# The y products of the RWKV steps, grouped by tile shape

## The chip, the cores and the metric

The kernel runs on one core of a Trainium2 chip. Its time is the device time of one execution in microseconds; the number that stands for a kernel is the median of its runs. The span is the time from the first to the last instruction of one profiled execution.

## The reference

One encoder layer on 256 tokens of width 2048, all in fp32. A combined projection of the normalised input feeds three things: a differential-attention group, an RWKV-7 group of 16 heads of 64 channels, and two merge gates. The two branches are projected, merged and added to the residual. Then a mixture of 16 experts with 32 tokens each follows.

The change lies in the RWKV-7 group. Each head has a 64x64 state S, scanned over the tokens once forward and once backward, and the two outputs are added:

```python
def step(S, inp):
    r_t, w_t, k_t, v_t, a_t, b_t = inp
    sa = jnp.einsum('bhvk,bhk->bhv', S, a_t)
    S = S * w_t[:, :, None, :] + sa[..., None] * b_t[:, :, None, :] + v_t[..., None] * k_t[:, :, None, :]
    return S, jnp.einsum('bhvk,bhk->bhv', S, r_t)
```

## The kernel before, in words

The scan is done in chunks of 64 tokens, four in sequence. Within a chunk the recurrence is solved with a triangular inverse, so a chunk needs a few matmuls of 64 columns. Heads are taken in four groups (`gp`, lines 612 to 630). A group has two head pairs (e), two heads per pair (h, in partitions 0 to 63 and 64 to 127, the slices `HH`), and two directions (d): eight scans side by side, which the list `eh` (line 533) runs through with h innermost.

For each group, three projections (`project_c`, lines 229 to 245) give r, k and v; `prep` (line 372) forms decays, the keys and the operands `X`, `rb`, `bt`, `vt_`; `invert` (line 474) forms `tt`, mainly by 62 small VectorE operations in sequence. `chain` (line 528) then runs the four sequential steps for the group before. A step c does the following:

- prr (line 557): eight products of the state tile `ss_` with `X[..., 0]`; ScalarE copies them to `rh` (559).
- pu (567): eight products of `tt` and `rh`; ScalarE and VectorE copy one head half each into `uu` (568, 569).
- psn (573), not in the last step: eight products of `bt` and `uu`; with the decayed state they become the next state `nsu` (574 to 580).
- py (583, 584): for each of the eight scans a product of `ss_` with `X[..., 1]`, contraction over 128 partitions, and then a product of `uu` with `rb`, contraction over 64 partitions, added to it. The two directions are then copied to `y` by ScalarE in steps 0 and 1 and added to it by VectorE in steps 2 and 3 (587, 589).

In the profile the first kind is the form 128\*64 (rows by columns of the array), the second 64\*64. Each fp32 matmul shows as two records, so eight matmuls are "x16".

prr, pu, psn and py are tiles of one PSUM pool, `chp`, with two banks (line 67). A new tile takes a bank when one is free, and an instruction that needs it waits until then. All eight banks of PSUM are given out to the pools of lines 63 to 67.

The order of the instructions on each engine is made when the kernel is built: a planner goes through them by priority and by its own model of their times (line 1013), and adds the semaphores. Weights' splits have priority 9000, `prep` and `invert` of group gp 10000 + 4000 gp, the chains 16000 and a term that grows with gp; a lower number goes first. The large projections, those of r, k and v and of the merge gates (`gates`, `GSCHED`), come behind all of these and fill the places between them. At run time each engine works through its own list in that order.

The projections' weights come through SyncE's queue in chunks of 512 KB and are split into a high and a low half (`wsplit`, lines 198 to 209) by ScalarE and VectorE (205, 206), two buffers for each half. After the RWKV groups come the attention, the branch projections, the output projection, the routing, and the experts (from line 882), whose weights are 1 MB loads into a ring of buffers (line 179).

Of the kernel before, what the change touches and what calls it, by code (L numbers as in the profile page):

```python
# [8 lines left out]
F32 = mybir.dt.float32  # L9
# [23 lines left out]

GSCHED = (1, 4, 1, 4, 6)    # gate projections behind each group of RWKV heads, and behind the last one
PS, PCH = 9000, 16000       # scheduling priorities: weights' splits; the heads' chunks in sequence
NEW, NE1, NEB = 14, 2, 8    # slots for the experts' weights: a ring, those of it free early, those used once
PACE = 3                    # chunks of other weights per early load of the experts'

# [14 lines left out]
def trunk_kernel(ctx, tc, x, attn_norm_g, w_in, q_norm_g, k_norm_g, lambda_q1, lambda_k1, lambda_q2,  # L53
# [4 lines left out]
    V, A, G, PE, SP = nc.vector, nc.scalar, nc.gpsimd, nc.tensor, nc.sync  # L58
# [8 lines left out]
    chp = tc.alloc_tile_pool(name="chp", bufs=2, space=PSUM)  # L67
# [37 lines left out]
    with ExitStack() as es:  # L105
# [29 lines left out]
        for kp in range(KT // 2):  # L135
# [5 lines left out]
            for i in range(2):  # L141
                kt = 2 * kp + i
                g = prm[:, 100 + kt:101 + kt]
# [3 lines left out]
    def pieces(q):  # L147
        """column pieces of the down projections; narrow ones at the very end"""
        return ((0, 1024), (1024, 1024)) if q < 3 else ((0, 1024), (1024, 512), (1536, 256), (1792, 256))
# [15 lines left out]
    def slot_of(i):  # L165
        """the pool of load i: the ring of NEW slots (NE1 of them free early), or the NEB that serve once"""
        if NEW <= i < NEW + NEB:
            return 2
        return int((i if i < NEW else i - NEB) % NEW >= NE1)
# [18 lines left out]
    def pace(wl):  # L188
        """ahead of the experts, a load of their weights for every few chunks of the stream"""
        i = len(ew_state["tiles"])  # L190
        if i == NEW or ew_state["pools"][slot_of(i)] is None:
            return
        ew_state["chunks"] += 1
        if ew_state["chunks"] % PACE == 0:
            with prio(2000000 + ew_state["chunks"]):
                fetch(wl[0:1, 0:1].bitcast(F32))
# [16 lines left out]
    def project_t(src, nk, c0, lh, ll, name, pool=None):  # L213
        """tokens on partitions: two banks [128 tok, 512]"""
        pool, tag = pool or (pjp, "pj")
        ps = [pool.tile([128, 512], F32, name=f"pj_{name}_{t}", tag=tag) for t in range(2)]
        for kc in range(nk // 2):
            wh, wl = wsplit(src[:, 2 * kc:2 * kc + 2, c0:c0 + 512], 2, 512, f"{name}_{kc}")
            for j in range(2):
                kt = 2 * kc + j  # L220
                for t in range(2):
                    s = slice(t * 128, (t + 1) * 128)
                    first, last = kt == 0, kt == nk - 1
                    PE.matmul(ps[t], lh[:, kt, s], wh[:, j], start=first, stop=False)  # L224
                    PE.matmul(ps[t], lh[:, kt, s], wl[:, j], start=False, stop=False)  # L225
                    PE.matmul(ps[t], ll[:, kt, s], wh[:, j], start=False, stop=last)  # L226
        return ps

    def project_c(src, nk, c0, width, rh, rl, name, pool=None):
        """channels on partitions: one bank [<=128 ch, 256 tok] per 128 columns"""  # L230
        nct = (width + 127) // 128
        pool, tag = pool or (pjp, "pj")
        ps = [pool.tile([128, T], F32, name=f"pc_{name}_{c}", tag=tag) for c in range(nct)]
        for kc in range(nk // 4):
            wh, wl = wsplit(src[:, 4 * kc:4 * kc + 4, c0:c0 + width], 4, width, f"{name}_{kc}")
            for c in range(nct):
                m = min(128, width - c * 128)
                for j in range(4):
                    kt = 4 * kc + j
                    first, last = kt == 0, kt == nk - 1  # L240
                    cs = slice(c * 128, c * 128 + m)
                    PE.matmul(ps[c][:m], wh[:, j, cs], rh[:, kt], start=first, stop=False)  # L242
                    PE.matmul(ps[c][:m], wh[:, j, cs], rl[:, kt], start=False, stop=False)  # L243
                    PE.matmul(ps[c][:m], wl[:, j, cs], rh[:, kt], start=False, stop=last)  # L244
        return ps
# [15 lines left out]

# [1 line left out]
    with ExitStack() as es:  # L263
# [71 lines left out]
        def head_norm(src, npair, scale, lo, eps, tag, pl_, pt_):  # L335
            """per-token, per-head rsqrt(max-or-add) of channel sums, spread back over the channels"""
            def tmp_(i):
# [34 lines left out]
        def prep(G_, e, r, k, v):  # L372
# [9 lines left out]
            SP.dma_start(w2s[64:128, 1], a2_b[0, :, chs])  # L382
            # decay and in-context rate
            pw = prepp.tile([128, 2, T], F32, name=f"pw{p}", tag="pr")
# [7 lines left out]
            for d in range(2):  # L392
                A.activation(ta[:, d], pa[:, d], AF.Tanh, bias=pch(44 + 8 * d), scale=0.5)
            # normalised keys
            kkr = r1.tile([128, T], F32, name="kkr", tag="kkr")
# [12 lines left out]
            V.tensor_copy(dec[:, 4:8], pp_[:, 4:8, 1])  # L408
            # the state's side of X: a | r of each head in its own half
            for h, hs in enumerate(HH):  # L410
# [11 lines left out]
            V.tensor_tensor(bk[:, :, 1], c8(ta), c8(cum), op=OP.mult)  # L422
            # products within the chunks: ab | rb in the head's half, ak | rk in the other half of X
            # (ab transposed for the backward scan)
            for d in range(2):
# [18 lines left out]
                for h in range(2):  # L444
                    ks = HH[1 - h]
                    V.tensor_tensor(X[ks, h, ns].rearrange("p n w t -> p n (w t)"), pK[ks],
                                    mk[ks, :, 128:256].to_broadcast([64, 4, 128]), op=OP.mult)
            # bonus, with the group norm's bias
            G.tensor_tensor(z, ta[:, 0], ta[:, 1], op=OP.add)
# [4 lines left out]
            G.tensor_scalar(z, z, pc(92), 1.0, op0=OP.add, op1=OP.mult)  # L454
            # values, and keys scaled to the chunk's end, with time on partitions
            pv = prepp.tile([128, 4, 64], F32, name=f"pv{p}", tag="pr")
# [17 lines left out]
        def invert(G_):  # L474
            """unit-triangular inverses: 32-blocks by substitution, blocks and row residues on partitions"""
            g, ab, tt = G_["g"], G_["ab"], G_["tt"]
# [51 lines left out]
        def chain(G_):  # L528
            """chunks in sequence, four scans side by side, then group norm, bonus and gate"""
            g = G_["g"]  # L530
# [4 lines left out]
            def stacked(c, name, eng):  # L535
                """a state's or a u's tile, the values of step c in its other half"""
                t = r2.tile([128, 2, 2, 2, 64], F32, name=name, tag=name)
# [6 lines left out]
            ss_, sd = None, None  # L544
            for c in range(4):
# [10 lines left out]
                for e, h, d in eh:  # L556
                    PE.matmul(prr[HH[h], e, d], X[:, e, h, ii[d], 0], ss_[:, e, h, d], start=True, stop=True)
                rh = r1.tile([128, 2, 2, 64], F32, name="rh")
                A.copy(rh, prr)
                if 0 < c < 3:  # L560
# [9 lines left out]
                if c < 3:  # L570
# [3 lines left out]
                    for h, hs in enumerate(HH):  # L574
# [4 lines left out]
                        else:  # L579
                            A.copy(nsu[hs, :, h], psn[hs])  # L580
                py = chp.tile([128, 2, 2, 64], F32, name=f"py{g}_{c}", tag="ch")
                for e, h, d in eh:
                    PE.matmul(py[HH[h], e, d], ss_[:, e, h, d], X[:, e, h, ii[d], 1], start=True, stop=False)
                    PE.matmul(py[HH[h], e, d], uu[HH[h], e, h, d], rb[HH[h], e, ii[d]], start=False, stop=True)
                for d in range(2):
# [51 lines left out]

# [1 line left out]
    hres = tc.alloc_tile_pool(name="hres", bufs=1, side=right)  # L639
# [7 lines left out]

# [1 line left out]
    ybr = tc.alloc_tile_pool(name="ybr", bufs=1, side=right)  # L649
# [18 lines left out]

# [1 line left out]
    with ExitStack() as es:  # L670
# [111 lines left out]

# [1 line left out]
    mg = tc.alloc_tile_pool(name="merged", bufs=1, side=left)  # L784
# [12 lines left out]

# [1 line left out]
    h = hrow  # L799
# [32 lines left out]

# [1 line left out]
    rt_ = ctx.enter_context(tc.tile_pool(name="route", bufs=1, side=left))  # L834
# [46 lines left out]

# [1 line left out]
    with ExitStack() as es:  # L883
        ewb = tc.alloc_tile_pool(name="ewb", bufs=NEB, side=left)
        ew_state["pools"][2] = ewb
        for q in range(4):
            es_ = slice(4 * q, 4 * q + 4)
            # one-hot rows of the slots: rstd folded in for the gather, the affinity for the scatter
            oh = e2.tile([128, 2, 4, CAP], F32, name="oh")
# [127 lines left out]
```

## Time and profile before

| what | us |
|---|---|
| median of three runs | 1905.14 |
| lowest and highest run | 1902.57, 1911.13 |
| span of the profiled execution | 1908.2 |
| TensorE busy (share) | 1718.0 (90%) |
| VectorE busy (share) | 702.0 (37%) |
| ScalarE busy (share) | 440.8 (23%) |
| GpSimd busy (share) | 192.7 (10%) |

The profiled execution is listed with its span alone, no other time of its own. The page is read from the totals down to single instructions: which engine is busy in which stretch, what it waits for there, and then the instructions that the change touches, one after another in order of time.

### The profile page before, as it was taken

To read this page: it belongs to the slowest core of one execution; us is meant where nothing else is said; L and a number is where in the kernel's file an instruction comes from. 1 tells how busy PE (TensorE), PEld (TensorE's weight loads), DVE (VectorE), ACT (ScalarE), POOL (GpSimd) and SP (SyncE) were. 2 spreads that over 40 slices of the span, in tenths; PEclk is the share of its full clock that TensorE was granted. 3 is DMA by queue.
4 is the path that set the end of the run, shared out by engine and by line. 5 is a ranking of instruction groups with operands and counts; after the bars stand their busy time and mean duration, and the time that the engine had idled before them with its cause. 6 is when DMAs were issued, how large, how long until landed. Compare 5 with 4: busy or idle time off the path is not lost.

```text
span 1908.2 us, 27455 instructions
## 1 busy us (share of the span) xinstructions
PE 1718.0 (90%) x11179; PEld 1059.7 (56%) x11179; DVE 702.0 (37%) x1524; ACT 440.8 (23%) x768; POOL 192.7 (10%) x295
## 2 busy tenths in 40 slices
PE   6999999999998899999979988978889888878877
PEld 6988888888987677998845222322223222211123
DVE  4678777696634667775430010000000000000000
ACT  6444444343333456544410000000000000000000
POOL 2342213332000331000000000000000000000000
PEclk9999999999999999999989999999999999999989
DMA  5655634355545665688899999999999999999997
GB/s 164 176 142 153 166 101 122 95 141 150 143 129 177 178 185 166 208 252 277 281 366 414 423 421 423 427 427 426 421 423 427 427 425 420 424 427 427 425 417 271
DMA packets 230383, 556.49 MB, mean 292 GB/s; under 512 B 40954, under 2 KB 138736, under 8 KB 197232
## 3 DMA queue, kind: packets, MB, share of 16 engines
q1 hardware_dynamic: 229904, 554.68, 78.7%
q8 instruction: 88, 1.44, 0.3%
q14 instruction: 39, 0.32, 0.0%
q0 software_dynamic: 352, 0.05, 0.0%
HBM read 543.14 MB, written 11.53 MB: 291 GB/s over the span
## 4 chain that ended last, share of the span: by engine, by line
DMA 36%; PE 25%; SPq 2%; DVE 1%; issue 1%; ACT 0%; POOL 0%; ACTq 0%; POOLq 0%; DVEq 0%
DMA w<-in_w_down_e_dram 13%; DMA w<-in_w_gate_e_dram 12%; DMA w<-in_w_up_e_dram 10%; PE pgu L920 5%; PE pd L954 4%; SPq L179 2%; PE pc_br L242 2%; PE pc_br L244 2%; PE pxe L903 2%; PE pc_br L243 2%; PE pj_wo L225 1%; PE pj_wo L226 1%; PE pj_wo L224 1%; PE pj_da L225 1%; PE pj_da L224 1%; PE pj_da L226 1%
## 5 line engine op out<-in xcount | busy, mean ns | idle before, releaser
L920 PE MATMUL pgu<-w,xe 128*32 128x512 f32 x2048 | 453.9, 603 | 65.8 <-DMA w<-in_w_gate_e_dram 32.5
L920 PEld LDWEIGHTS pgu<-w,xe 128*32 128x32 f32 x2048 | 109.8, 110 | 393.7 <-issue 230.2
L954 PE MATMUL pd<-w,hdT 128*32 128x512 f32 (+1 forms) x1088 | 245.4, 592 | 56.5 <-DMA w<-in_w_down_e_dram 55.6
L954 PEld LDWEIGHTS pd<-w,hdT 128*32 128x32 f32 x1088 | 64.7, 111 | 233.7 <-DMA w<-in_w_down_e_dram 122.9
L242 PE MATMUL pc_gt<-xh,wh_gt 128*128 128x256 f32 x512 | 149.7, 295 | 0.0
L244 PE MATMUL pc_gt<-xh,wl_gt 128*128 128x256 f32 x512 | 144.8, 294 | 5.2 <-DVE wl_gt L206 5.0
L243 PE MATMUL pc_gt<-xl,wh_gt 128*128 128x256 f32 x512 | 146.6, 289 | 0.0
L935 ACT ACTIVATE th<-pgu 128x512 f32<-128x512 f32 x8 | 4.8, 597 | 519.0 <-PE pgu L920 519.0
L904 DVE TENSOR_TENSOR xe<-pxe,fg 128x512 f32<-128x512 f32 x16 | 11.0, 690 | 295.0 <-PE pgu L920 241.7
L242 PE MATMUL pc_rkv<-xh,wh_rkv 128*128 128x256 f32 x384 | 111.1, 292 | 2.0 <-ACT wh_rkv L205 2.0
L243 PE MATMUL pc_rkv<-xl,wh_rkv 128*128 128x256 f32 x384 | 111.8, 293 | 0.0
L244 PE MATMUL pc_rkv<-xh,wl_rkv 128*128 128x256 f32 x384 | 108.5, 293 | 1.1 <-DVE wl_rkv L206 1.1
L963 DVE TENSOR_TENSOR acc<-poe,acc 128x512 f32<-128x512 f32 (+1 forms) x26 | 16.9, 651 | 247.3 <-PE poe L962 247.3
L244 PEld LDWEIGHTS pc_gt<-xh,wl_gt 128*128 128x128 f32 x512 | 96.7, 194 | 9.4 <-DVE wl_gt L206 7.0
L242 PEld LDWEIGHTS pc_gt<-xh,wh_gt 128*128 128x128 f32 x512 | 99.7, 195 | 3.3 <-issue 1.2
L243 PEld LDWEIGHTS pc_gt<-xl,wh_gt 128*128 128x128 f32 x512 | 99.9, 195 | 1.6 <-issue 1.1
L936 DVE SCALAR_TENSOR_TENSOR th<-th,pgu 128x512 f32<-128x512 f32 x8 | 5.5, 688 | 249.8 <-ACT th L935 216.4
L206 DVE TENSOR_TENSOR wl_gt<-raw_gt,wh_gt 128x1024 fp32r<-128x1024 f32 x64 | 79.7, 1246 | 43.2 <-ACT wh_gt L205 43.1
L205 ACT CAST wh_gt<-raw_gt 128x1024 fp32r<-128x1024 f32 x64 | 67.0, 1046 | 100.3 <-PE pc_gt L243 81.4
L225 PE MATMUL pj_da<-wl_da,xh 128*128 128x512 f32 x192 | 78.4, 408 | 6.9 <-DVE wl_da L206 6.8
L958 ACT COPY ye<-pd 128x512 f32<-128x512 f32 (+1 forms) x17 | 9.5, 561 | 311.0 <-PE pd L954 311.0
L206 DVE TENSOR_TENSOR wl_da<-raw_da,wh_da 128x1024 fp32r<-128x1024 f32 x48 | 63.6, 1324 | 37.7 <-ACT wh_da L205 37.2
(385 smaller groups left out, 2964.8 us busy)
## 6 DMA issues: line engine op xcount, KB each, us to landing
w<-in_w_gate_e_dram SPq DMA_DIRECT2D x128, 1024.0 KB, 19.5
w<-in_w_up_e_dram SPq DMA_DIRECT2D x128, 1024.0 KB, 19.6
w<-in_w_down_e_dram SPq DMA_DIRECT2D x128, 1024.0 KB, 18.1
raw_gt<-in_w_in_dram SPq DMA_DIRECT2D x64, 512.0 KB, 3.9
raw_rkv<-in_w_in_dram SPq DMA_DIRECT2D x48, 512.0 KB, 3.9
raw_da<-in_w_in_dram SPq DMA_DIRECT2D x48, 512.0 KB, 3.7
raw_wo<-in_w_out_dram SPq DMA_DIRECT2D x32, 512.0 KB, 5.5
raw_br<-in_w_branch_b_dram SPq DMA_DIRECT2D x16, 512.0 KB, 4.0
```

Of the source, the lines that this page charges most:

```text
L179: SP.dma_start(w, src)
L205: A.copy(wh[:, :n], raw[:, :n])
L206: V.tensor_tensor(wl[:, :n], raw[:, :n], wh[:, :n].bitcast(F32), op=OP.subtract)
L224: PE.matmul(ps[t], lh[:, kt, s], wh[:, j], start=first, stop=False)
L225: PE.matmul(ps[t], lh[:, kt, s], wl[:, j], start=False, stop=False)
L226: PE.matmul(ps[t], ll[:, kt, s], wh[:, j], start=False, stop=last)
L242: PE.matmul(ps[c][:m], wh[:, j, cs], rh[:, kt], start=first, stop=False)
L243: PE.matmul(ps[c][:m], wh[:, j, cs], rl[:, kt], start=False, stop=False)
L244: PE.matmul(ps[c][:m], wl[:, j, cs], rh[:, kt], start=False, stop=last)
L903: PE.matmul(px[:, j], h[:, t, kt::KT], ohr[:, t], start=t == 0, stop=t == 1)
L920: PE.matmul(pgu[2 * gu + hf][js], xe[kt // 4][:, kt % 4, js], wt[2 * j + gu][:, k, hf * 512:(hf + 1) * 512], start=kt == 0, stop=kt == KT - 1)
L954: PE.matmul(pd[nb][js], hT[:, ft, js], wt[j][:, k, nb * nw:(nb + 1) * nw], start=ft == 0, stop=ft == 7)
```

## The change

The state products of a step are issued right behind prr, as one run of eight; the u products stay in their place behind psn, as a second run of eight. The bank of py is therefore taken at the start of the step. The start flag, which clears a bank's marks for the partitions that the matmul writes, is set only on the first two state products (one in each half of the partitions), and the stop flag on the last two u products. Operands, outputs and the number of matmuls are the same. The diff also drops comments and docstrings, which is not shown.

```diff
                 for e, h, d in eh:
                     PE.matmul(prr[HH[h], e, d], X[:, e, h, ii[d], 0], ss_[:, e, h, d], start=True, stop=True)
                 rh = r1.tile([128, 2, 2, 64], F32, name="rh")
+                py = chp.tile([128, 2, 2, 64], F32, name=f"py{g}_{c}", tag="ch")
+                for k_, (e, h, d) in enumerate(eh):
+                    PE.matmul(py[HH[h], e, d], ss_[:, e, h, d], X[:, e, h, ii[d], 1], start=k_ < 2, stop=False)
                 A.copy(rh, prr)
...
-                py = chp.tile([128, 2, 2, 64], F32, name=f"py{g}_{c}", tag="ch")
-                for e, h, d in eh:
-                    PE.matmul(py[HH[h], e, d], ss_[:, e, h, d], X[:, e, h, ii[d], 1], start=True, stop=False)
-                    PE.matmul(py[HH[h], e, d], uu[HH[h], e, h, d], rb[HH[h], e, ii[d]], start=False, stop=True)
+                for k_, (e, h, d) in enumerate(eh):
+                    PE.matmul(py[HH[h], e, d], uu[HH[h], e, h, d], rb[HH[h], e, ii[d]], start=False, stop=k_ > 5)
                 for d in range(2):
                     if c < 2:
                         A.copy(y[:, :, nn[d]], py[:, :, d])
```

## Rows read from the trace of the kernel before

**Rows 1.** The page, totals: engine, busy us, share of the span, instructions.

```profile
span 1908.2 us, 27455 instructions
PE 1718.0 (90%) x11179; PEld 1059.7 (56%) x11179; DVE 702.0 (37%) x1524; ACT 440.8 (23%) x768; POOL 192.7 (10%) x295
```

**Rows 2.** Busy time by stretch: length, PE, PEld, DVE, ACT, POOL, clock, DMA share, GB/s.

```profile
140.00:220.00 80.00, 75.18 (x752) 69.09 (x751) 67.74 (x161) 35.05 (x58) 16.41 (x21) 1.00 0.64 170
220.00:600.00 380.00, 374.49 (x3879) 330.71 (x3879) 252.61 (x580) 142.25 (x255) 82.88 (x123) 0.97 0.47 125
300.00:500.00 200.00, 195.87 (x2106) 172.41 (x2099) 144.51 (x338) 73.72 (x135) 51.40 (x76) 0.97 0.46 122
...
1040.00:1908.00 868.00, 732.87 (x3134) 215.01 (x3134) 42.65 (x66) 19.70 (x36) 0.00 (x0) 0.98 1.00 415
```

**Rows 3.** Waits of PE, 200 to 1000 us: total us, times, longest.

```profile
PE pj_da L225 <- DVE wl_da L206: 6.8, 4, 3.9
...
PE pc_gt L244 <- DVE wl_gt L206: 2.6, 4, 1.2
```

**Rows 4.** Chain of waits, a stretch of the experts: start us, us, what.

```profile
1222.01 19.56 DMA w<-in_w_up_e_dram
```

**Rows 5.** Timeline of PE, one step's y products: start us, us, line, out<-in.

```profile
256.09 0.33 PE L583 MATMUL py<-X,su 128*64 128x64 f32 x2
256.35 0.33 PE L584 MATMUL py<-rb,uu 64*64 64x64 f32 x2
...
259.68 0.50 PE L244 MATMUL pc_rkv<-xh,wl_rkv 128*128 128x256 f32 x2
```

**Rows 6.** Busy time by stretch, instructions on the tile py alone: PE, PEld, DVE, ACT.

```profile
220.00:600.00 380.00, 67.35 (x512) 48.75 (x512) 3.99 (x16) 3.46 (x16) 0.97 0.47 125
```

**Rows 7.** Timeline of PE, psn and the instruction behind it.

```profile
223.85 0.69 PE L573 MATMUL psn<-uu,bt 128*64 128x64 f32 x16
224.36 0.28 PE L583 MATMUL py<-X,su 128*64 128x64 f32 x2
```

**Rows 8.** Timeline of PE, prr and pu, each with the instruction behind it.

```profile
262.14 0.69 PE L557 MATMUL prr<-su,X 128*64 128x64 f32 x16
...
262.75 0.39 PE L244 MATMUL pc_rkv<-xh,wl_rkv 128*128 128x256 f32 x1
...
265.34 0.68 PE L567 MATMUL pu<-rh,tt 64*64 64x64 f32 x16
...
265.95 0.33 PE L583 MATMUL py<-X,su 128*64 128x64 f32 x2
...
266.21 0.38 PE L244 MATMUL pc_rkv<-xh,wl_rkv 128*128 128x256 f32 x1
```

**Rows 9.** Tile py: ns min/median/max of an instruction; who waited for it (us, times).

```profile
L583 PE MATMUL py<-X,su x256: 222/222/367, 224.4 to 582.5; 128*64 128x64 f32 x128
...
  ACT su L541: 24.9, 8
```

**Rows 10.** Stretches with line 583 alone: PE, PEld, clock; first and last of four.

```profile
240.00:250.00 10.00, 2.55 (x16) 1.43 (x14) 0.83 0.14 38
...
540.00:550.00 10.00, 0.00 (x0) 0.00 (x0) 0.83 0.32 84
```

**Rows 11.** Timeline of PE, projections behind a block of y products, and later.

```profile
244.83 0.41 PE L244 MATMUL pc_rkv<-xh,wl_rkv 128*128 128x256 f32 x1
245.04 0.41 PE L242 MATMUL pc_rkv<-xh,wh_rkv 128*128 128x256 f32 x1
...
247.77 0.28 PE L243 MATMUL pc_rkv<-xl,wh_rkv 128*128 128x256 f32 x1
247.88 0.28 PE L244 MATMUL pc_rkv<-xh,wl_rkv 128*128 128x256 f32 x1
```

**Rows 12.** Waits of DVE, 220 to 600 us: total us, times, longest.

```profile
DVE wl_rkv L206 <- ACT wh_rkv L205: 17.1, 11, 6.9
DVE y L589 <- PE py L584: 14.0, 6, 3.2
```

## The prediction

> **What bounds the kernel now.** I read the page's totals first. TensorE is busy for 1718 of the 1908.2 us [rows 1], but that is a mean over stages with different limits, so the second view is the busy time by stretch. The changed lines run only between 224 and 583 us. From 220 to 600 us PE is busy 374.5 of 380 us, while DVE has 252.6 and ACT 142.3, and the DMA share is 0.47 [rows 2]. The third view asks what PE waits for: from 200 to 1000 us the longest entry in the list is 6.8 us, and the largest wait inside the changed stretch is 2.6 us for the low halves of the gate weights [rows 3]. So in this stretch PE is the bound, and PE time that is really removed moves everything behind it forward.
>
> From 1040 us on the DMA engines are full at a share of 1.00 and PE has 733 of 868 us [rows 2]; the chain of waits there is one expert weight after another, 19.56 us each [rows 4]. That stage is as long as its bytes. It doesn't hide a gain made before it, because its loads wait for buffers and code that come after the RWKV stage: it begins sooner and lasts as long. A gain in 220 to 600 us should reach the end nearly whole.
>
> **The y products today.** Each of the 16 steps (4 groups by 4 chunks) issues 8 pairs: a state product on the 128\*64 form (line 583), then a u product on the 64\*64 form (line 584). Each matmul is two fp32 passes, so a step is 16 pieces "x2". In the timeline the pieces alternate and start 0.256 us apart: from 256.09 to 259.68 us there are 14 pieces, 3.59 us [rows 5]. One step thus holds PE for 16 x 0.256 = 4.10 us, and 16 steps for 65.6 us. The busy time of the tile py gives 67.35 us from the other side; it counts the tail of each last matmul [rows 6]. A few pieces continue a run of the same form before them and cost less, so I take 65.
>
> **The same matmuls in one form.** Three products of the same step show it. The 16 passes of psn (128\*64) start at 223.85 and the next same-form instruction at 224.36: 0.51 us [rows 7]. Those of prr (128\*64) start at 262.14 and a projection follows at 262.75: 0.61 us. Those of pu (64\*64) start at 265.34, and the next form at 265.95: 0.61 us [rows 8]. These are exactly the two forms of the y products, with the same moving size of 64 columns. The price today is therefore the change of form between pieces, not the arithmetic: a single pass has the same median of 0.222 us in the alternation [rows 9].
>
> **What the change does to it.** The number of matmuls stays at 16 passes of each form per step; no copy is added.
> - First run (state products): it now stands right behind prr, which reads the same state and has the same form. Between 0.51 us (joined to prr) and 0.61 us (alone). I take 0.55.
> - Second run (u products): 0.61 us if whole. The planner cuts runs today where half of u comes late; one pair cut off and surrounded by projections holds 0.26 us, as at 265.95 us [rows 8]. So 0.61 to 0.87, and I take 0.70, nearer the whole run, since pu is whole in the same place.
> - Sum per step 1.25 us, for 16 steps 20 us. Removed: 65 - 20 = 45 us. Bounds: 65.6 - 16 x 1.12 = 47.7 and 65 - 16 x 1.48 = 41.3 us.
> - The start flag on two matmuls in place of eight, and the stop flag, change no instruction; I cost them at nothing, because flags ride on matmuls that are issued anyway.
>
> The two heads' u products sit in different row halves of the array and write one bank; pu does the same today, and its 16 passes leave room for the next form after 0.61 us [rows 8]. The Trainium skill ("TensorEngine Tiling (Array Packing)", Restrictions and Gotchas) says that different row tiles cannot access the same PSUM bank simultaneously, and that software must keep them apart. By the row the second run costs 0.61 us, by that rule up to 16 x 0.22 = 3.5 us. The trace doesn't bear the rule out for tiles that also lie in different column halves, and I go by the row.
>
> **The clock.** In five places the granted clock is at its lower level, 1.2 GHz, for a part of a slice: slices at 0.83 in 240 to 250, twice in 350 to 370, 490 to 500 and 540 to 550 us [rows 10]. Each begins at the end of, or within half a microsecond behind, a block of alternating y products; the projections behind the first then start 0.21 us apart in place of 0.12 [rows 11]. A slice at 0.83 loses 1.7 us, so five cost 8.5. The uniform runs of 0.6 us don't show this in their wake. Without the 4 us blocks I expect most of it back: 0 to 8.5 us, I take 6.
>
> **What is late next.** PE gets 51 us less work in 380, so other engines come closer. In the densest part, 300 to 500 us, DVE has 144.5 us of work; the eight steps of two groups run there, so 200 - 8 x 2.8 - 5 (three of the clock's places) = 173 us remain, 84% DVE. The nearest case is 140 to 220 us: DVE 67.7 of 80 us (85%), and PE is busy 75.2 there, 6% lost [rows 2]. If that held over 300 to 500 us, some 10 us would be lost; if the cover holds, as now, nothing. I take 6.
>
> **The moved waits.** ACT waits 24.9 us in 8 places for the state products before it can refill a state buffer [rows 9]; with the products early, these go. ACT isn't the bound, so I count nothing. The added wait: py now takes one of the pool's two banks from the start of the step to the y copies, where pu took it before. pu must wait for rh's copy out of prr's bank, psn for u's copy out of pu's bank; both wait for that data today. Only the next step's first run waits for something new, the y copies. Queued behind it on PE are pu and the projections. Today DVE stands ready for the y sums and waits for PE, 14.0 us in 6 places [rows 12], so the copies come at once; nothing counted.
>
> **Sum.** -45 - 6 + 6 = -45 us. The profiled span is 1908.2 us, 3.1 above the median of 1905.14, and no other time is listed for that execution; 1908.2 - 45 = 1863.2 there, and 1860 beside the median.
>
> **Rivals.**
> - Half is lost (0.09): the order on every queue is planned anew at build, and DVE, with its splits, falls behind PE; DVE already waits for ACT, 6.9 us at the longest [rows 12]. For: 84% DVE. Against: DVE's waits are mostly for engines that wait for PE. Gain 23 us, 1882.
> - The change doesn't do what it says (0.06): the planner cuts the runs into pairs between projections. Each pair then costs a change of form, 0.26 us again, and only half the clock loss returns: 1896 to 1907, say 1901. Against: prr and pu, traced the same way, are mostly whole.
> - The late bank (0.05), the slower side: the first run stands in PE's order ahead of pu, and if the y copies sit on DVE behind a split that waits for ACT, PE stands still in the 12 steps that have one before them. It decides from 51 / 12 = 4.3 us per step; at 5.5 us it is 66 us and the time 1905 - 51 + 66 = 1920. Against: [rows 12] shows DVE early.
> - Row halves kept apart in one bank (0.02): 16 x (3.5 - 0.7) = 45 us of the gain go, about 1905.
>
> **How the numbers follow.** The forecast has 0.78; its own spread is 1848 (all 47.7 and 8.5 us, no new wait) to 1876 (41.3, no clock, 10 us of waits, and the spread of the runs shown, 1902.6 to 1911.1). To hold eight in ten with some weight for the second case the range is 1848 to 1884. A measurement can tell 0.5% (9.5 us) from no change. Faster: 0.78 + 0.09 + half of 0.06 = 0.90; same 0.03 + 0.02 = 0.05; slower 0.05.
>
> **What would show it.** Right: tile py busy near 22 us for 512 passes (32 runs of 0.69 us, the last tail counted), rows "x16" or longer for both lines, the slices at 0.83 gone or fewer, PE still above 93% until the RWKV steps end, and the stage from the first expert weight to the end as long as now. Wrong: pieces "x2" in the y products, PE waits for low halves or for y copies of more than 15 us in total, or an expert stage that grew by what the front lost.

## The result and the profile after

The changed kernel takes 1878.32 us (median; 1875.99 to 1878.9) beside 1908.14 us for the kernel before on the same chip: ratio 0.9842, 95% interval 0.9824 to 0.9861. The forecast was 1860 us in 1848 to 1884. The direction and the main term were right; the gain is 30 us in place of 45.

The page of the changed kernel, totals (columns as in [rows 1]):

```profile
span 1876.0 us, 27452 instructions
PE 1679.5 (90%) x11179; PEld 1032.0 (55%) x11179; DVE 701.4 (37%) x1524; ACT 440.4 (23%) x768; POOL 189.9 (10%) x295
```

PE has as many instructions as before and 38.5 us less busy time. The span is 32.2 us shorter, so somewhere PE also gained idle time.

The timeline of PE, one step of the changed kernel, answers to [rows 5], [rows 7] and [rows 8]:

```profile
311.34 0.69 PE L557 MATMUL prr<-su,X 128*64 128x64 f32 x16
311.86 0.64 PE L563 MATMUL py<-X,su 128*64 128x64 f32 x16
312.43 1.13 PE L390 MATMUL pa<-lora,w2s 128*128 128x512 f32 x2
```

```profile
255.31 0.67 PE L587 MATMUL py<-rb,uu 64*64 64x64 f32 x14
255.92 0.39 PE L243 MATMUL pc_rkv<-xl,wh_rkv 128*128 128x256 f32 x1
```

The first run joins prr, 0.52 us behind its start, and gives way after 0.57 us. The second holds PE for 0.61 us, here without one pair (x14). That pair stands ahead of it between projections and holds PE for 0.25 us by itself:

```profile
252.46 0.32 PE L587 MATMUL py<-rb,uu 64*64 64x64 f32 x2
252.71 0.39 PE L244 MATMUL pc_rkv<-xh,wl_rkv 128*128 128x256 f32 x1
```

The second run is cut in this way in 14 of the 16 steps. The two forms of the y products do not alternate any more. Busy time on the tile py alone (answers to [rows 6]; it begins at 130 us, because the first step's state products are now issued at 140 us):

```profile
130.00:600.00 470.00, 27.57 (x512) 21.53 (x512) 3.91 (x16) 3.48 (x16) 0.97 0.54 148
```

67.35 has become 27.57 us. To see what became of these 39.8 us, both traces are read over two stretches: from 101 us to the end of the gate projections, and from the start to the first expert matmul. First the kernel before, then the changed one; columns as in [rows 2]:

```profile
101.00:588.00 487.00, 474.97 (x4935) 424.54 (x4934) 342.75 (x774) 190.92 (x339) 115.82 (x163) 0.98 0.50 132
...
0.00:982.60 982.60, 928.50 (x7701) 815.46 (x7702) 654.94 (x1451) 420.71 (x731) 192.70 (x295) 0.97 0.59 175
```

```profile
101.00:562.00 461.00, 434.49 (x4937) 398.56 (x4936) 345.66 (x790) 190.30 (x338) 113.88 (x163) 0.97 0.52 140
...
0.00:949.60 949.60, 884.64 (x7700) 785.02 (x7700) 654.50 (x1451) 420.30 (x731) 189.88 (x295) 0.98 0.61 181
```

Up to the end of the gates PE is busy 40.5 us less (474.97 to 434.49), and idle 14.5 us more (12.0 to 26.5): the stretch is 26.0 us shorter. But it is not quite the same work: the last matmuls of the last head group start at 599.3 us in the kernel before, behind the gates, and at 559.2 us in the changed one, ahead of their end. Up to the first expert matmul the work is the same. There PE is busy 43.9 us less (928.50 to 884.64) and idle 10.9 us more (54.1 to 65.0): 33.0 us. From the first expert matmul to the end it is 926.4 us, 925.6 before: as forecast, that stage passes the gain on. 33.0 - 0.8 = 32.2 us, the difference of the spans.

The new idle time is told by the waits of PE from 101 to 562 us, the five largest (total us, times, longest):

```profile
PE psn L578 <- DVE uu L574: 5.3, 2, 5.1
PE pc_rkv L244 <- DVE wl_rkv L206: 3.9, 4, 1.9
PE pz L452 <- DVE X L446: 3.0, 2, 1.6
PE py L587 <- ACT uu L573: 2.2, 2, 1.6
PE pz L452 <- DVE xx L494: 2.2, 1, 2.2
```

The largest was not there before. DVE's timeline around it:

```profile
448.89 0.22 DVE L492 TENSOR_TENSOR tmp<-xx,dd 128x62 f32<-128x62 f32 x1 [7.54 <-DMA dd<-scn]
...
453.33 0.43 DVE L574 COPY uu<-pu 64x256 f32<-64x256 f32 x1
```

The copy of u that psn needs stands on DVE behind the next group's inverse. That inverse waited 7.5 us for a DMA, so the copy came at 453.33 us, and psn started at 453.81, although ScalarE had copied its half of u at 444.96.

The granted clock did not come back either (line 563 alone: PE, PEld, clock, DMA share, GB/s):

```profile
150.00:160.00 10.00, 0.00 (x0) 0.00 (x0) 0.83 0.38 106
240.00:250.00 10.00, 0.64 (x16) 0.55 (x16) 0.83 0.37 107
300.00:310.00 10.00, 0.00 (x0) 0.00 (x0) 0.69 0.27 65
390.00:400.00 10.00, 0.00 (x0) 0.00 (x0) 0.91 0.31 85
450.00:460.00 10.00, 0.00 (x0) 0.00 (x0) 0.66 0.18 52
```

These five slices lose 10 x (0.17 + 0.17 + 0.31 + 0.09 + 0.34) = 10.8 us, no less than the 8.5 us of before [rows 10]. But they have another neighbour: read in slices of 0.1 us, the level falls at 152.5, 241.3, 299.3, 398.3 and 452.9 us, each time in a wait of PE or at most 1.3 us behind one.

```profile
152.48 0.58 PE L244 MATMUL pc_rkv<-xh,wl_rkv 128*128 128x256 f32 x1 [1.86 <-DVE wl_rkv L206]
...
240.85 0.27 PE L587 MATMUL py<-rb,uu 64*64 64x64 f32 x1 [1.55 <-ACT uu L573]
...
297.99 0.45 PE L452 MATMUL pz<-z,crw 128*128 128x256 f32 x1 [1.56 <-DVE X L446]
...
395.96 0.67 PE L452 MATMUL pz<-z,crw 128*128 128x256 f32 x2 [2.18 <-DVE xx L494]
397.50 0.68 PE L459 MATMUL pv<-cst,rkv 64*64 64x64 f32 x16 [0.88 <-DVE tmp L492]
...
453.81 0.70 PE L578 MATMUL psn<-uu,bt 128*64 128x64 f32 x8 [5.14 <-DVE uu L574]
```

The kernel before has one such place as well, which the prediction's five leave out: its level falls at 437.8 us, behind this wait and without a block of y products near it.

```profile
436.65 1.20 PE L511 MATMUL ph<-tst,ab 32*32 32x32 f32 x64 [1.70 <-DVE tst L501]
...
430.00:440.00 10.00, 0.00 (x0) 0.00 (x0) 0.89 0.95 237
```

### The profile page after: what moved, and what is told of

Same layout as the page of the kernel before. It is cut to its first block, busy times and chain, and to the rows that moved or that the text cites. A ratio compares the mean times of both kernels' runs of the same rounds, so it can differ in the third digit from the quotient of the medians.

```text
span 1876.0 us, 27452 instructions
## 1 busy us (share of the span) xinstructions
PE 1679.5 (90%) x11179; PEld 1032.0 (55%) x11179; DVE 701.4 (37%) x1524; ACT 440.4 (23%) x768; POOL 189.9 (10%) x295
## 4 chain that ended last, share of the span: by engine, by line
DMA 35%; PE 27%; SPq 2%; DVE 1%; issue 1%; ACT 0%; POOL 0%; ACTq 0%; POOLq 0%; DVEq 0%
DMA w<-in_w_down_e_dram 13%; DMA w<-in_w_gate_e_dram 11%; DMA w<-in_w_up_e_dram 11%; PE pgu L923 6%; PE pd L957 4%; SPq L179 2%; PE pxe L906 2%; PE pc_br L242 2%; PE pc_br L244 2%; PE pj_wo L225 2%; PE pc_br L243 2%; PE pj_wo L226 2%; PE pj_wo L224 2%; PE pj_da L225 1%; PE pj_da L224 1%; PE pj_da L226 1%
## 5 line engine op out<-in xcount | busy, mean ns | idle before, releaser
L923 PE MATMUL pgu<-w,xe 128*32 128x512 f32 x2048 | 458.6, 610 | 63.4 <-DMA w<-in_w_gate_e_dram 31.6
L907 DVE TENSOR_TENSOR xe<-pxe,fg 128x512 f32<-128x512 f32 x16 | 11.0, 690 | 296.4 <-PE pgu L923 241.3
```

The costliest lines, as they stand in the source:

```text
L923: PE.matmul(pgu[2 * gu + hf][js], xe[kt // 4][:, kt % 4, js], wt[2 * j + gu][:, k, hf * 512:(hf + 1) * 512], start=kt == 0, stop=kt == KT - 1)
```

## The experiments

All ratios are to the kernel before, run beside each kernel. The planner makes a new order for every edit, which matters below. "Idle" is PE's idle time, worked out as above from each kernel's trace. The expectations count it from 101 us to the end of the gates; kernels are compared over the same work, from the start to the first expert matmul. There it is 54.1 us in the kernel before and 65.0 us in the changed one.

**Is the price the change of form?** In the kernel before, a u product also follows the state product that it adds to, at the same place in PSUM; a wait there would look the same. Two kernels tell these apart; both have their y products behind psn, as the kernel before, and the start flags of the changed kernel. Of their diffs only the new loop is shown. The first keeps the alternation, but lets each u product follow the state product of the next scan:

```diff
+                for k_ in range(9):
+                    if k_ < 8:
+                        e, h, d = eh[k_]
+                        PE.matmul(py[HH[h], e, d], ss_[:, e, h, d], X[:, e, h, ii[d], 1], start=k_ < 2, stop=False)
+                    if k_ > 0:
+                        e, h, d = eh[k_ - 1]
+                        PE.matmul(py[HH[h], e, d], uu[HH[h], e, h, d], rb[HH[h], e, ii[d]], start=False, stop=k_ > 6)
```

> The two forms alternate as before, but each u product follows the state product of the next scan, so neighbours write different places in the bank: 14 pieces per step in place of 16. If the change of form is the price, pieces start 0.26 us apart, the y products hold PE for some 57 us and the ratio to before is 0.995 to 1.0. If the price before was a product that waits for the one before it at the same place in PSUM, they fall to 20 to 30 us and the ratio to 0.984 to 0.988.

Measured: 1901.19 us, ratio 0.9959 (0.9943 to 0.9975). Its timeline of PE and its busy time on the tile py:

```profile
243.03 0.33 PE L590 MATMUL py<-rb,uu 64*64 64x64 f32 x2
243.28 0.33 PE L587 MATMUL py<-X,su 128*64 128x64 f32 x2
243.54 0.33 PE L590 MATMUL py<-rb,uu 64*64 64x64 f32 x4
243.80 0.39 PE L242 MATMUL pc_rkv<-xh,wh_rkv 128*128 128x256 f32 x1
```

```profile
220.00:600.00 380.00, 60.47 (x512) 44.00 (x512) 4.00 (x16) 3.31 (x16) 0.97 0.46 128
```

The pieces still start 0.25 us apart, though neighbours write different places; the last piece, with two products, holds PE no longer than one with one. The wait at one place in PSUM is out, and so are the start flags as the cause of the gain. The second kernel has half the changes of form:

```diff
+                for k_ in range(0, 8, 2):
+                    for e, h, d in eh[k_:k_ + 2]:
+                        PE.matmul(py[HH[h], e, d], ss_[:, e, h, d], X[:, e, h, ii[d], 1], start=k_ < 2, stop=False)
+                    for e, h, d in eh[k_:k_ + 2]:
+                        PE.matmul(py[HH[h], e, d], uu[HH[h], e, h, d], rb[HH[h], e, ii[d]], start=False, stop=k_ > 5)
```

> State products of both heads of a pair and direction, then their u products: 8 pieces of 4 passes per step in place of 16 of 2. If each change of form has a fixed price, a piece holds PE for about 0.26 + 0.06 us, the y products for some 41 us in all, and the ratio to before is near 0.990. If the price is the wait at the same place in PSUM, one other product lies between and the y products fall to 20 to 30 us, ratio 0.984 to 0.988.

Measured: 1878.6 us, ratio 0.9846 (0.983 to 0.9862). The tile py in its trace:

```profile
220.00:600.00 380.00, 38.24 (x512) 27.78 (x512) 4.00 (x16) 3.31 (x16) 0.98 0.52 145
```

Busy time on py is 67.35 us at 16 pieces per step, 60.47 at 14, 38.24 at 8 and, in the next kernel, 24.21 at 2. It grows with the number of pieces at equal work: (67.35 - 38.24) / (16 x 8) = 0.23 us per piece from 8 to 16 pieces, (38.24 - 24.21) / (16 x 6) = 0.15 us from 2 to 8. (The second run is cut in some steps, so 2 is the least.) The pairs were somewhat cheaper than I expected (38 for 41 us).

Their time is not the one that I expected, however: the ratio is 0.9846 in place of 0.990, in the range of the other theory and as low as the changed kernel's. The tile py, 38 us and not 20 to 30, still speaks against that theory. Up to the first expert matmul:

```profile
0.00:952.40 952.40, 894.55 (x7701) 789.93 (x7702) 655.01 (x1451) 419.62 (x731) 190.60 (x295) 0.98 0.59 181
```

PE is busy 9.9 us more than in the changed kernel, near the 10.7 us more on py. It is idle 7.1 us less (57.9 us), and the experts take 2.8 us less (923.6). So this plan has the changed kernel's time with half of the changes of form left.

**Was the gain lost by issuing the state products early?** Both runs go back behind psn, where the y products stood; the bank is then taken late, too.

```diff
-                py = chp.tile([128, 2, 2, 64], F32, name=f"py{g}_{c}", tag="ch")
-                for k_, (e, h, d) in enumerate(eh):
-                    PE.matmul(py[HH[h], e, d], ss_[:, e, h, d], X[:, e, h, ii[d], 1], start=k_ < 2, stop=False)
                 A.copy(rh, prr)
...
+                py = chp.tile([128, 2, 2, 64], F32, name=f"py{g}_{c}", tag="ch")
+                for k_, (e, h, d) in enumerate(eh):
+                    PE.matmul(py[HH[h], e, d], ss_[:, e, h, d], X[:, e, h, ii[d], 1], start=k_ < 2, stop=False)
                 for k_, (e, h, d) in enumerate(eh):
                     PE.matmul(py[HH[h], e, d], uu[HH[h], e, h, d], rb[HH[h], e, ii[d]], start=False, stop=k_ > 5)
```

> Both runs stand behind psn, where the y products stood before; two uniform runs, the bank taken late as before. If taking the bank and the state products early (or the new order that this makes) brought the 14 us of new PE idle time, that idle time falls back to about 12 us ahead of the end of the gate projections and the time is near 1864 us, ratio to before 0.977. If the idle time comes from the other engines now being close whatever the place of the first run, idle stays near 26 us and the ratio near 0.984. The tile py holds PE for 22 to 26 us in both.

Measured: 1868.97 us, ratio 0.9794 (0.9777 to 0.981), faster than the changed kernel. Its stretch to the end of the gates and its tile py:

```profile
101.00:550.00 449.00, 429.77 (x4935) 393.67 (x4934) 343.73 (x773) 189.85 (x339) 119.37 (x163) 0.98 0.53 144
```

```profile
220.00:600.00 380.00, 24.21 (x512) 20.48 (x512) 3.90 (x16) 3.36 (x16) 0.97 0.53 150
```

Idle is 449.0 - 429.8 = 19.2 us there, between the two theories' numbers, and 7 us less than in the changed kernel. But the end of the last head group lies behind the gates here, as in the kernel before. Up to the first expert matmul idle is 62.5 us, 2.5 less than in the changed kernel. The changed kernel with one edit elsewhere speaks against a price of the early place:

```diff
                 A.copy(uu[HH[0], :, 0], pu[HH[0]])
-                V.tensor_copy(uu[HH[1], :, 1], pu[HH[1]])
+                A.copy(uu[HH[1], :, 1], pu[HH[1]])
```

> The changed kernel, with the second half of u copied by ScalarE in place of VectorE. If the longest new wait (5.1 us, psn for the u copy that stood on VectorE behind the inverse, which waited for a DMA) is a true loss, PE's waits for the VectorE copy of u (5.3 us) go, idle falls to about 18 to 20 us and the ratio to before goes from 0.984 to about 0.980. If PE's idle time is set by the weights' splits and only changes its name, another wait takes its place and the ratio stays 0.984.

Measured: 1868.54 us, ratio 0.9787 (0.9769 to 0.9805), idle 20.5 us to the end of the gates and 62.9 us to the first expert matmul. The wait for VectorE's copy is gone from its list (101 to 549 us is 448.0 us, PE busy 427.5):

```profile
101.00:549.00 448.00, 427.46 (x4940) 392.22 (x4939) 335.73 (x758) 196.58 (x355) 115.57 (x163) 0.99 0.53 144
```

So the early run (1868.54 us) is no dearer than the late one (1868.97 us) once that wait is away. Both edits together:

> Both runs behind psn, and the second half of u copied by ScalarE. If the early first run costs time only through the one long wait for VectorE's copy of u, that wait is gone in either version alone and the two don't add: ratio to before 0.976 to 0.981, idle of PE near 19 us. If the place of the run and the engine of the copy are two separate costs of some 10 us each, the ratio is near 0.974 and idle falls to 10 to 14 us.

Measured: 1866.92 us, ratio 0.9766 (0.9746 to 0.9785), the lowest median of all, but its interval overlaps those of the two alone. PE's idle time to the first expert matmul is 62 to 63 us in each of the three; two separate costs of 10 us are not seen.

To take the place of the run and the luck of one plan apart, both placements were built from another order of the same eight scans, and the changed kernel was run again beside them:

```diff
-            eh = [(e, h, d) for e in range(2) for d in range(2) for h in range(2)]
+            eh = [(e, h, d) for d in range(2) for e in range(2) for h in range(2)]
```

With the early run:

> The changed kernel with the eight scans listed direction first, then head pair: the same work in every product, another order that the planner starts from. If the early place of the first run costs some 9 us as such, this one stays near the changed kernel, ratio 0.982 to 0.986, and 0.004 or more above the next. If the 9 us came from how that one plan fell out, it lands anywhere from 0.976 to 0.987.

With both runs late:

> Both runs behind psn, with the same other order of the scans. If the late place is better as such, the ratio is 0.977 to 0.981, at least 0.004 below the one with the early run. If plans differ by luck, the difference between the two is under 0.003 or turns round.

The changed kernel again:

> The changed kernel once more, beside the two, so that the comparison doesn't rest on another chip: ratio 0.982 to 0.987.

Measured: early 1867.6 us, ratio 0.9798 (0.9778 to 0.9818); late 1868.83 us, 0.9806 (0.9785 to 0.9827); the changed kernel 1875.16 us, 0.984 (0.9819 to 0.9862). The late place is not better as such: the difference turns round. The changed kernel's slower time repeats, so it belongs to its plan. The five others, up to the first expert matmul, in the order of their runs above (late; copy on ScalarE; both; early and late with the other order):

```profile
0.00:944.90 944.90, 882.39 (x7700) 784.25 (x7700) 655.77 (x1451) 419.69 (x731) 195.16 (x295) 0.98 0.60 182
0.00:942.40 942.40, 879.47 (x7697) 781.40 (x7697) 647.77 (x1435) 425.92 (x747) 191.96 (x295) 0.98 0.60 183
0.00:941.20 941.20, 879.08 (x7697) 780.05 (x7697) 646.52 (x1435) 425.69 (x747) 192.93 (x295) 0.98 0.60 183
0.00:944.10 944.10, 879.78 (x7697) 782.67 (x7697) 655.19 (x1451) 419.88 (x731) 192.08 (x295) 0.98 0.60 182
0.00:941.60 941.60, 881.01 (x7700) 782.31 (x7700) 655.26 (x1451) 419.48 (x731) 194.51 (x295) 0.98 0.60 183
```

They are 4.7 to 8.4 us shorter than the changed kernel's 949.6: 2.2 to 5.6 us less busy and 0.6 to 4.4 us less idle. None of them has the wait of 5.1 us for u, but in each a part of it comes back as other waits.

**Is VectorE's load what holds PE now?** Every second round of the inverse's substitution is left out, 30 of 62 VectorE operations per group, in the late kernel and in the kernel before.

```diff
-            for j in range(31):
+            for j in range(0, 31, 2):
```

> Both runs behind psn, and every second round of the inverse's substitution is left out (31 operations of VectorE per group in place of 62, so the inverse isn't complete). If VectorE's load is what holds PE once the y products are short, PE's idle time ahead of the end of the gates falls from 18.9 to some 12 us, as before, and the ratio goes from 0.979 to 0.975 or below. If the idle time comes from the order and from single latencies, it stays and the ratio is 0.978 to 0.981.

> The kernel before, with every second round of the inverse's substitution left out. TensorE was its bound by either theory, so 35 us less work on VectorE changes nothing: ratio 0.996 to 1.002. If VectorE already held it, the ratio is under 0.994.

Measured: late 1877.7 us, ratio 0.9825 (0.9804 to 0.9847); before 1918.55 us, ratio 1.004 (1.0023 to 1.0057). Less work made neither faster: the kernel before became slower by 0.4%; for the late kernel the ratio rose from 0.9794 to 0.9825, with intervals that touch. Up to the first expert matmul, first the late kernel, then the one before, each with half the substitution; and the latter to the end of its gates:

```profile
0.00:948.60 948.60, 882.23 (x7697) 782.76 (x7697) 628.65 (x1331) 419.34 (x731) 190.89 (x295) 0.98 0.60 181
0.00:995.20 995.20, 939.42 (x7701) 826.73 (x7703) 627.65 (x1331) 420.61 (x731) 186.69 (x295) 0.96 0.57 173
...
101.00:608.70 507.70, 491.27 (x4957) 440.21 (x4955) 320.65 (x673) 192.04 (x342) 111.23 (x163) 0.95 0.47 128
```

VectorE has 27 us less in the late one, and PE's idle time rises from 62.5 to 66.4 us: less load did not lower it. (The test takes off 4% of VectorE's work up to the experts, 655.8 to 628.7 us, not more.) That it comes from the order and from single latencies is what remains; no run varies these alone. In the kernel before the clock falls to 0.95 up to the gates where it had 0.98, and PE is busy 10.9 us longer for the same matmuls.

## Why the prediction was right, and where its sizes failed

- *PE is the bound from 220 to 600 us, and the experts pass the gain on*: right. Busy time fell by 43.9 us up to the first expert matmul, and the experts took 0.8 us more than before.
- *The price is the change of form*: right, and shown by the two kernels that vary it at equal work. One reading under it was too wide: [rows 9] give the 0.222 us of a state product. A u product does last longer in the alternation, 0.267 us at the median and 0.218 in the run (first the kernel before, then the changed one):

```profile
L584 PE MATMUL py<-rb,uu x256: 218/267/366, 226.3 to 582.7; 64*64 64x64 f32 x128
...
L587 PE MATMUL py<-rb,uu x256: 218/218/366, 226.2 to 542.5; 64*64 64x64 f32 x128
```

- *65 - 20 = 45 us*: nearly. Busy time on py fell by 39.8 us, below the low bound of 41.3. The term that was too small is the second run. I took 0.70 us, near the whole run, but in 14 of 16 steps a pair is cut off: 0.25 + 0.61 = 0.86 us, about the upper end that I had given. In the busy time, 27.57 us where I had 22, the 14 pieces of 0.32 us make 4.5 us; much of the rest is two second runs at the lower clock. This is a small part of the rival in which the planner cuts the runs into pairs.
- *The second run writes one bank from two row halves at the price of pu*: right, 0.61 us in the row above. No run here bears out the limit that the Trainium skill states for row tiles ("TensorEngine Tiling (Array Packing)", Restrictions and Gotchas) for tiles that also differ in their column half.
- *The clock gives back 6 us*: failed. In the RWKV steps nothing came back: all slices of 10 us under 1.00 up to the end of the gates, from 101 us on, lose 12.0 us together, 10.2 before. The blocks of alternation went, and with them the slices behind them; new ones came beside PE's new waits. I had taken one neighbour of the lower clock for its only one, though the place at 437.8 us stood in the same trace. Outside the RWKV steps the slices from 20 to 30 and from 610 to 650 us lost 6.8 us before; the changed kernel loses 1.7 us there, from 570 to 580 us. (Both lose some right ahead of the experts.) The change does not touch that work and the forecast did not mean it, so this part of the gain is luck.
- *6 us of new waits, from VectorE's load*: failed in size and in cause. It was 10.9 us up to the experts (14.5 more to the end of the gates, 3.6 less elsewhere), and leaving out half of the inverse's substitution did not lower it in the late kernel. What grew are single waits in a fixed order: the work planned between two instructions no longer covers a DMA or a copy that comes late. The longest, 5.1 us, is of the kind of the late-bank rival (a copy that stands on VectorE behind something else), but at u, not at y.
- *The moved wait costs nothing*: right. No first run waits for the y copies in the changed kernel; built from another order, the early and the late place differ by no more than their intervals.
- *The sum*: busy time up to the experts fell by 43.9 us where I had 45 + 6, which is 7.1 us too much, 5.2 of them at the y products; idle grew by 10.9 where I had 6, 4.9 us too little; the experts took 0.8. -45 + 7.1 + 4.9 + 0.8 = -32.2 us, the span.

Still open is what in a change of form takes the time: the weight loads of the tile py shrink with it (PEld 48.75 us at 16 pieces, 20.48 in the late kernel), and no run separates the loads from the products. Open, too, is why the changed kernel is 8 or 9 us slower than four neighbours. The wait of 5.1 us is gone in all of them, but their idle time up to the experts is only 0.6 to 4.4 us lower; the rest is busy time and the stage of the experts (922.5 to 924.4 us there, 926.4 here), and every edit re-planned everything else as well.

## What to carry to other kernels

Where small matmuls of different tile shapes share a stage that TensorE bounds, look at the distance between their starts, not at their own durations: 0.22 us for a state product in both cases, but 0.26 us per piece alternating and 0.6 us for a whole run of 16. Sort them by shape, also across accumulations in one bank. (The Trainium skill, "TensorEngine Tiling (Array Packing)", Tiling Modes, says that a change of tiling mode drains TensorE; the 0.15 to 0.23 us per piece agree with it.) When an order is planned at build, a gain of 2% comes with some 0.4% of luck; build the same change from two or three equivalent orders before saying which part of it costs something.

## What the runs showed that I had not expected

The lower clock has two kinds of neighbour here: with no wait of PE in sight, the ends of the 4 us blocks in which forms alternate (five of 16 blocks in the kernel before); and waits of PE (once up to the gates in the kernel before, five times in the changed kernel). Neither is always followed by it: in the kernel before PE also stood still for 2.0 us up to 151.6 us, and the slice from 150 to 160 us is at 1.00. And 30 VectorE operations less per group made the kernel before slower, by 0.4%.
